# Values of the last two groups of heads by seven half-size products instead of eight

## Chip, core and metric

One core of one Trainium2 chip. The metric is the device time of one execution in microseconds (us), median of the runs shown. Engines: TensorE (PE, with its weight loads as PEld), VectorE (DVE), ScalarE (ACT), GpSimd (POOL), SyncE (SP, which issues most of the DMAs here).

## What is computed

Two layers on a sequence of 512 tokens of width 1024, float32. Layer 0 is a pooling mixer, layer 1 an HGRN2 mixer. Cut to layer 1:

```python
u = h @ w_in                                   # (512, 1024) @ (1024, 8192)
q, fz, i, gate = jnp.split(u, 4, axis=-1)      # each (512, 2048): 16 heads of 128
log_f = jnp.logaddexp(jnp.log(lbf), jnp.log1p(-lbf) + jax.nn.log_sigmoid(fz))
k = (1.0 - lbf) * jax.nn.sigmoid(-fz)
...
o = hgrn2_chunk_scan(qc, kc, vc, bc)           # vc is i, cut into chunks
o = o * lax.rsqrt(jnp.mean(o * o, axis=-1, keepdims=True) + EPS)
...
return (o * jax.nn.silu(gate)) @ w_out
```

`h` is normed before the product; the kernel multiplies by the gain of the norm before it, and by the tokens' factor (`rn`) after it. The values `i` of two groups of heads together are one product of 512 tokens x 1024 inputs by 1024 inputs x 1024 columns.

## The kernel before

Every large product has float32 operands that are split into a high and a low part (`split`, L95 to L97: ACT casts the high part, DVE subtracts it for the low one). Each product of a 128x128 stationary tile and a 128x512 moving tile is then three matmuls (`mm3`, L127 to L130). Weights come in pieces of 512 KB (`piece`, L99 to L107): one DMA on SP's queue into a raw tile `wraw` (three of them, `RAW = 3`), then ACT's cast into `whi` and DVE's subtraction into `wlo` (six pairs, `WB = 6`). A piece holds two of the eight slices of 128 inputs, for 512 columns. These three instructions stand in `tc.high_priority`, so that they are placed some 300 instructions early. The program is a plain list of instructions; a planner orders them for each engine when the program is built, by priority and by its own estimate of when operands and tiles are free, and each engine then runs its list in that order. Tiles with one `tag` share that tag's buffers, and a tile waits until an earlier one with its buffer has had its last reader.

Layer 1 (`hgrn`, L349) works on four groups of four heads (`NG = 4`, `GC = 512` columns a group). For each group:
- `prepare(g)` (L548): `forget` (96 matmuls, with sigmoids and scans of products on DVE) and `queries` (96 matmuls). For each head it ends in a reciprocal on DVE (L572), two products for k on POOL (L574, L575) and two for q on DVE (L576, L577). It runs after the first two heads of the group before have been gated (`gated`, L461), and ahead of the other two.
- `inputs(g)` (L422): the values, in four blocks of 128 tokens, 24 matmuls each (eight slices x three), 96 in all. ACT scales each block by `rn` out of PSUM (L430) into `v` (tag `vn`, one buffer).
- `within` (L580) for each head: four matmuls k by q, a masked copy into `Ads` on DVE (L590, L591), three transposes of k. `state` (L599): three matmuls by `v` and updates on DVE.
- for groups 1 and 2, `add_out` (L381): the output product of the group before, eight halves of 12 matmuls, each added to `ht` on DVE (L379); then `attend` for four heads (L618) and `gates1` (96 matmuls). Group 0 has `turn` (L365, transposes h into `ht`) and the gates around the attention; group 3 has the gates around the attention, and `add_out` of group 2 at its end. `finish` (L503) does the last output product, the norm and the stores.

PSUM has four buffers for the large products (tag `mm`) and four for the small ones (tag `a`). Two groups of small SBUF tiles matter below: `hg` and `sq`, with two buffers each, which sigmoids, gates and norms share; and `f` (two buffers, 2 x 512 elements), which `prepare` holds until its last reciprocal has been used.

```python
def group(g, prepare, heads, zs):
    first, last = g == 0, g == NG - 1
    attend = heads(g, inputs(g))
    ...
    now = [gated(g, n, ons[n], gts[n], last) for n in range(2)]
    if not last:
        prepare(g + 1)
    now += [gated(g, n, ons[n], gts[n], last) for n in range(2, GT)]
    if last:
        add_out(load_out(w1_out, g - 1), zs)
    return now
```

## Time and profile before

| | |
|---|---|
| median of 3 runs | 828.1 us (828.09 to 828.32) |
| profiled execution, device time | 828.94 us |
| its span, first to last instruction | 827.1 us |
| mean granted TensorE clock | 0.997 |
| busy: PE, PEld, DVE, ACT, POOL | 816.1, 685.8, 546.2, 278.7, 150.3 us |
| DMA | 81.14 MB, mean 98 GB/s |

Times of rows are us from the start of the span unless they say ns. A matmul is shown from its start to a modelled end, and the next one begins before that: a run of 128x512 matmuls is to be timed by the distance of the starts. The same holds for DVE and ACT, whose instructions overlap by some 0.1 us.

### The profile page before, as it was taken

To read this page: it belongs to the slowest core of one execution; us is meant where nothing else is said; L and a number is where in the kernel's file an instruction comes from. 1 tells how busy PE (TensorE), PEld (TensorE's weight loads), DVE (VectorE), ACT (ScalarE), POOL (GpSimd) and SP (SyncE) were. 2 spreads that over 40 slices of the span, in tenths; PEclk is the share of its full clock that TensorE was granted. 3 is DMA by queue.
4 is the path that set the end of the run, shared out by engine and by line. 5 is a ranking of instruction groups with operands and counts; after the bars stand their busy time and mean duration, and the time that the engine had idled before them with its cause. 6 is when DMAs were issued, how large, how long until landed. Compare 5 with 4: busy or idle time off the path is not lost.

```text
span 827.1 us, 10198 instructions
## 1 busy us (share of the span) xinstructions
PE 816.1 (99%) x3902; PEld 685.8 (83%) x3902; DVE 546.2 (66%) x837; ACT 278.7 (34%) x476; POOL 150.3 (18%) x197
## 2 busy tenths in 40 slices
PE   9999999999999999999999999999999999999995
PEld 8888888888888888888888888888888888888884
DVE  5687537854785465798169973359973459973744
ACT  7442134223234244325342241343240333242311
POOL 0030010002011032260313400313300313302100
PEclk9999999999999999999999999999999999999998
DMA  9531324223232155133033240333240333240302
GB/s 342 198 103 52 101 102 153 78 71 116 94 101 103 55 178 178 52 102 102 1 102 102 77 128 1 103 102 102 77 128 1 103 101 102 77 126 3 102 14 92
DMA packets 37769, 81.14 MB, mean 98 GB/s; under 512 B 2896, under 2 KB 3152, under 8 KB 37712
## 3 DMA queue, kind: packets, MB, share of 16 engines
q1 hardware_dynamic: 35264, 76.56, 28.3%
q10 hardware_dynamic: 2448, 3.86, 1.3%
q8 instruction: 32, 0.52, 0.3%
q14 instruction: 25, 0.20, 0.1%
HBM read 76.21 MB, written 4.19 MB: 97 GB/s over the span
## 4 chain that ended last, share of the span: by engine, by line
PE 95%; DVE 3%; issue 1%; DMA 0%; ACT 0%; POOLq 0%; POOL 0%; DVEq 0%; ACTq 0%
PE mm L128 29%; PE mm L129 28%; PE mm L130 28%; PE a L625 2%; PE a L627 1%; PE a L588 1%; PE a L605 1%; DVE r L572 1%; PE a L466 1%; DVE wlo L97 1%; PE a L83 1%; PE a L594 0%; DMA wraw<-in_w1i 0%; PE a L128 0%; PE a L130 0%
## 5 line engine op out<-in xcount | busy, mean ns | idle before, releaser
L128 PE MATMUL mm<-xh,whi 128*128 128x512 f32 x624 | 244.7, 392 | 0.0
L129 PE MATMUL mm<-xl,whi 128*128 128x512 f32 x624 | 243.2, 390 | 0.0
L130 PE MATMUL mm<-xh,wlo 128*128 128x512 f32 x624 | 243.0, 390 | 0.0
L96 ACT CAST whi<-wraw 128x1024 fp32r<-128x1024 f32 (+1 forms) x140 | 141.8, 1026 | 237.3 <-PE mm L129 108.6
L97 DVE TENSOR_TENSOR wlo<-wraw,whi 128x1024 fp32r<-128x1024 f32 (+1 forms) x140 | 172.0, 1253 | 56.6 <-ACT whi L96 54.5
L130 PEld LDWEIGHTS mm<-xh,wlo 128*128 128x128 f32 x624 | 117.3, 188 | 24.6
L128 PEld LDWEIGHTS mm<-xh,whi 128*128 128x128 f32 x624 | 117.4, 188 | 24.1 <-DVE h L222 0.3
L129 PEld LDWEIGHTS mm<-xl,whi 128*128 128x128 f32 x624 | 117.3, 188 | 24.2
L572 DVE RECIPROCAL r<-r 128x512 f32<-128x512 f32 x16 | 53.4, 3338 | 0.0
L128 PE MATMUL mm<-whi,xh 128*128 128x512 f32 x128 | 50.1, 391 | 0.0
L129 PE MATMUL mm<-wlo,xh 128*128 128x512 f32 x128 | 50.0, 391 | 0.0
L130 PE MATMUL mm<-whi,xl 128*128 128x512 f32 x128 | 49.9, 390 | 0.0
L129 PE MATMUL mm<-zl,whi 128*128 128x512 f32 x128 | 49.8, 389 | 0.0
L128 PE MATMUL mm<-zh,whi 128*128 128x512 f32 x128 | 49.8, 389 | 0.0
L130 PE MATMUL mm<-zh,wlo 128*128 128x512 f32 x128 | 49.8, 389 | 0.0
L379 DVE TENSOR_TENSOR ht<-mm,ht 128x512 f32<-128x512 f32 x32 | 22.0, 688 | 35.1 <-PE mm L130 35.1
L222 DVE TENSOR_TENSOR h<-mm,h 128x512 f32<-128x512 f32 x32 | 21.9, 688 | 28.4 <-PE mm L130 28.1
L442 POOL TENSOR_TENSOR gs<-fz,s 128x512 f32<-128x512 f32 x16 | 21.5, 1342 | 98.7 <-ACT s L440 98.7
L299 POOL TENSOR_TENSOR gs<-gt,sg 128x512 f32<-128x512 f32 x16 | 21.9, 1372 | 87.8 <-ACT sg L297 87.8
L128 PE MATMUL mm<-whi,z1h 128*128 128x512 f32 x96 | 37.6, 392 | 0.0
L130 PE MATMUL mm<-whi,z1l 128*128 128x512 f32 x96 | 37.4, 390 | 0.0
L129 PE MATMUL mm<-wlo,z1h 128*128 128x512 f32 x96 | 37.4, 389 | 0.0
(151 smaller groups left out, 1156.0 us busy)
## 6 DMA issues: line engine op xcount, KB each, us to landing
wraw<-in_w1i SPq DMA_DIRECT2D x64, 512.0 KB, 3.9
wraw<-in_w0i SPq DMA_DIRECT2D x28, 512.0 KB, 4.3
wraw<-in_w0o SPq DMA_DIRECT2D x16, 512.0 KB, 3.7
wraw<-in_w1o SPq DMA_DIRECT2D x16, 512.0 KB, 4.3
wraw<-in_w0g SPq DMA_DIRECT2D x8, 512.0 KB, 3.9
h<-in_xT SPq DMA_DIRECT2D x8, 256.0 KB, 5.1
wraw<-in_w0i SPq DMA_DIRECT2D x8, 256.0 KB, 5.3
xt<-in_x SPq DMA_DIRECT2D x4, 512.0 KB, 6.7
```

The source lines that it names most:

```text
L83: nc.tensor.matmul(warm[:, :P], ones, ones, start=True, stop=True)
L96: nc.scalar.copy(out=hi, in_=src)
L97: nc.vector.tensor_tensor(out=lo, in0=src, in1=hi, op=ALU.subtract)
L128: nc.tensor.matmul(out, lh, rh, start=start, stop=False)
L129: nc.tensor.matmul(out, lh, rl, start=False, stop=False)
L130: nc.tensor.matmul(out, ll, rh, start=False, stop=stop)
L222: nc.vector.tensor_tensor(out=h[n], in0=acc, in1=h[n], op=ALU.add)
L299: nc.gpsimd.tensor_tensor(out=gs, in0=gt, in1=sg, op=ALU.mult)
L379: nc.vector.tensor_tensor(out=ht[b][:, c], in0=acc, in1=ht[b][:, c], op=ALU.add)
L442: nc.gpsimd.tensor_tensor(out=gs, in0=gt, in1=sg, op=ALU.mult)
L572: nc.vector.reciprocal(out=r, in_=r)
L625: nc.tensor.matmul(o[:, b], Ads[pr][:, j, t], v[:, b, n * P:(n + 1) * P], start=True, stop=b == 0)
```

## The change

For the values of groups 2 and 3 the product X (tokens x inputs) by W (inputs x columns) is cut into 2 x 2 blocks: X into two halves of 256 tokens and two of 512 inputs, W into two halves of inputs and the 512 columns of either group. Seven products of sums of blocks (each two blocks of 128 tokens, four slices of inputs: 24 matmuls) take the place of eight. All seven run in group 2, in `inputs2`; sums of X are made in group 0 (`differences`), written to DRAM, and read back (`again`) into the buffers of `h`; sums of W are made on DVE from raw pieces. The values of group 3 go to DRAM (`v_d`) and `inputs(3)` only reads them. In the last group the output product of group 2 is cut into blocks that stand between the other parts, and half of the gates stand between `within` and `state`. The diff, cut to its core:

```diff
+    h = [const.tile([P, T], F32, name=f"h{k}", tag=f"h{k}", bufs=1) for k in range(KD)]
...
+        own = [[(hi[:, t:t + 256], lo[:, t:t + 256]) for hi, lo in xs[k:k + 4]] for t in (0, 256) for k in (0, 4)]
+        sums_d = dram.tile([2, 4, P, 2, T], F32, name=f"sums_{name}")
+        v_d = dram.tile([TB, P, GC], F32, name=f"v_{name}")
...
+        def differences():
+            for j in range(4):
+                t0, t4 = (small.tile([P, T], F32, name="t", tag="hg", bufs=2) for _ in range(2))
+                for t, k in ((t0, j), (t4, 4 + j)):
+                    nc.scalar.activation(out=t, in_=h[k], func=AF.Copy, scale=pp[:, C_NG1 + k:C_NG1 + k + 1])
+                d, e = (small.tile([P, T], F32, name="d", tag="sq", bufs=2) for _ in range(2))
...
+                first = halves(d, "z1", 4, l1)
+                second = [const.tile([P, T], F32R, name="s", tag=f"h{k}", bufs=1) for k in (j, 4 + j)]
+                split(e, *second)
+                for i, pair in enumerate((first, second)):
+                    for c, x in enumerate(pair):
+                        nc.scalar.dma_start(out=sums_d[i, j, :, c], in_=x.bitcast(F32))
+
+        def again(i):
+            out = []
+            for j in range(4):
+                x = const.tile([P, 2, 256], F32R, name="s", tag=f"h{4 * (i % 2) + j}", bufs=1)
+                nc.sync.dma_start(out=x.bitcast(F32), in_=sums_d[i // 2, j, :, :, (i % 2) * 256:(i % 2) * 256 + 256])
...
+        def inputs2(g):
...
+            def load(*a):
+                raw = wpool.tile([P, 2, GC], F32, name="wraw", tag="wraw", bufs=RAW)
+                with tc.high_priority(AHEAD):
+                    nc.sync.dma_start(out=raw, in_=block(*a))
+                return raw
+            def add(out, x, y):
+                with tc.high_priority(AHEAD):
+                    nc.vector.tensor_tensor(out=out, in0=x, in1=y, op=ALU.add)
+                return out
...
+            def product(accs, x, pieces):
+                for b, acc in enumerate(accs):
+                    t = slice(b * P, (b + 1) * P)
+                    for k, ((xh, xl), (wh, wl)) in enumerate(zip(x, pieces)):
+                        mm3(acc, xh[:, t], xl[:, t], wh, wl, k == 0, k == 3)
+            two = lambda: [ps.tile([P, T], F32, name="mm", tag="mm", bufs=4) for _ in range(2)]
...
+            a = two()
+            product(a, own[0], cut(load(0, 0, 0)) + cut(load(0, 0, 1)))
+            for b in range(2):
+                nc.scalar.copy(out=v[:, 2 + b], in_=a[b])
+            a = two()
+            product(a, own[1], cut(load(1, 0, 0)) + cut(load(1, 0, 1)))
+            for b in range(2):
+                plus(v[:, b], a[b], v[:, 2 + b])
+                times(v[:, b], rn, b)
+            pieces = []
+            for i in range(2):
+                x, y = load(0, 0, i), load(0, 1, i)
+                chain.append(l1.tile([P, 2, GC], F32, name="chain", tag="f", bufs=2))
+                pieces += cut(add(chain[i], x, y))
+            c = two()
+            product(c, s(0), pieces)
+            s2 = s(1)
+            pieces = [x for i in range(2) for x in cut(add(chain[i], chain[i], load(1, 1, i)))]
+            a = two()
+            product(a, s2, pieces)
+            s3 = s(2)
+            for b in range(2):
+                plus(v1[b], a[b], v[:, 2 + b])
+            pieces = []
+            for i in range(2):
+                x, y = load(0, 1, i), load(1, 1, i)
+                pieces += cut(add(x, x, y))
+            a = two()
+            product(a, s3, pieces)
+            s4 = s(3)
+            for b in range(2):
+                plus(v[:, 2 + b], a[b], v1[b])
+                plus(v1[2 + b], c[b], v[:, 2 + b])
+                plus(v1[b], c[b], v1[b])
+                times(v1[2 + b], nrn, 2 + b)
+                nc.scalar.dma_start(out=v_d[2 + b], in_=v1[2 + b])
+            pieces = [x for i in range(2) for x in cut(add(chain[i], chain[i], load(1, 0, i)))]
+            a = two()
+            product(a, own[3], pieces)
+            for b in range(2):
+                plus(v[:, 2 + b], a[b], v[:, 2 + b])
+                times(v[:, 2 + b], rn, 2 + b)
+            a = two()
+            product(a, s4, cut(load(1, 1, 0)) + cut(load(1, 1, 1)))
+            for b in range(2):
+                plus(v1[b], a[b], v1[b])
+                times(v1[b], nrn, b)
+                nc.scalar.dma_start(out=v_d[b], in_=v1[b])
+            return v
...
-            attend = heads(g, inputs(g))
-            if first:
+            v = inputs(g)
+            if last:
+                wg = load_in(w1_in, 3 * DI + g * GC)
+                gts = gates1(wg, (0, 1))
+                attend = heads(g, v, lambda: gts.extend(gates1(wg, (2, 3))))
+                wo = load_out(w1_out, g - 1)
+                add_out(wo, zs, (0,))
+                ons = [attend(n) for n in range(GT)]
+                add_out(wo, zs, (1,))
+            elif first:
+                attend = heads(g, v)
                 turn()
-            if first or last:
+                differences()
...
             if last:
-                add_out(load_out(w1_out, g - 1), zs)
+                add_out(wo, zs, (2, 3))
             return now
...
                 kts = [within(n) for n in range(GT)]
+                if mid:
+                    mid()
                 sts = [state(g, n, kts[n], v) for n in range(GT)]
```

`plus` is a DVE addition of a PSUM tile and an SBUF tile, `times` an ACT scaling in place, `cut` the split of a tile into a `whi` and a `wlo`. In each `j` of `differences` the part left out is four DVE operations on 256 columns.

## Rows read from the trace of the kernel before

**Rows 1.** The page, its busy line and the granted clock in 40 slices.
```profile
PE 816.1 (99%) x3902; PEld 685.8 (83%) x3902; DVE 546.2 (66%) x837; ACT 278.7 (34%) x476; POOL 150.3 (18%) x197
...
PEclk9999999999999999999999999999999999999998
```
**Rows 2.** Waits of PE, 310 to 828 us: total us, times, longest.
```profile
PE a L594 <- ACT kt L596: 0.3, 1, 0.3
PE a L605 <- DVE Ad L591: 0.2, 1, 0.2
```
**Rows 3.** PE in order of time: first and last matmul of group 2's values, 96 in all.
```profile
589.45 0.47 PE L128 MATMUL mm<-whi,xh 128*128 128x512 f32 x1
...
611.33 0.39 PE L130 MATMUL mm<-whi,xl 128*128 128x512 f32 x1
```
**Rows 4.** Stretches: length, busy PE, PEld, DVE, ACT, POOL, clock, DMA share, GB/s.
```profile
567.00:590.00 23.00, 23.00 (x107) 19.12 (x106) 23.00 (x31) 5.27 (x6) 10.88 (x13) 1.00 0.30 92
590.00:612.00 22.00, 22.00 (x100) 18.01 (x99) 17.45 (x18) 7.57 (x10) 3.18 (x2) 1.00 0.33 103
612.00:619.50 7.50, 7.50 (x68) 7.46 (x67) 6.85 (x18) 3.30 (x6) 0.00 (x0) 1.00 0.79 261
619.50:641.00 21.50, 21.50 (x97) 17.75 (x96) 8.83 (x22) 1.87 (x2) 0.00 (x0) 1.00 0.00 1
...
715.00:736.30 21.30, 21.30 (x96) 17.59 (x95) 16.64 (x18) 7.32 (x9) 3.17 (x2) 1.00 0.34 105
```
**Rows 5.** DVE in order of time, 587 to 613 us: start, us, line, operation.
```profile
587.80 3.34 DVE L572 RECIPROCAL r<-r 128x512 f32<-128x512 f32 x1
591.07 3.96 DVE L97 TENSOR_TENSOR wlo<-wraw,whi 128x1024 fp32r<-128x1024 f32 x3
594.95 0.68 DVE L418 TENSOR_TENSOR q<-mm,rb 128x512 f32<-128x512 f32 x1
595.55 0.41 DVE L576 TENSOR_TENSOR q<-q,r 128x256 f32<-128x256 f32 x1
595.88 0.41 DVE L577 TENSOR_TENSOR q<-q,f 128x256 f32<-128x256 f32 x1
596.22 3.34 DVE L572 RECIPROCAL r<-r 128x512 f32<-128x512 f32 x1
599.49 1.15 DVE L97 TENSOR_TENSOR wlo<-wraw,whi 128x1024 fp32r<-128x1024 f32 x1
600.56 0.95 DVE L576 TENSOR_TENSOR q<-q,r 128x256 f32<-128x256 f32 x1
601.44 0.41 DVE L577 TENSOR_TENSOR q<-q,f 128x256 f32<-128x256 f32 x1
601.77 1.40 DVE L468 SCALAR_TENSOR_TENSOR z<-a,pp,gs 128x512 f32<-128x512 f32 x2
603.20 1.35 DVE L97 TENSOR_TENSOR z1l<-z,z1h 128x512 fp32r<-128x512 f32 x2
608.80 3.95 DVE L97 TENSOR_TENSOR wlo<-wraw,whi 128x1024 fp32r<-128x1024 f32 x3 [4.25 <-ACT whi L96]
```
**Rows 6.** The tile `wraw`, 560 to 660 us: from a DMA's issue to its landing.
```profile
DMA to landing us min/median/max: 3.5/3.8/4.7
```
**Rows 7.** ACT in order of time, 595 to 604 us; in brackets the idle time before.
```profile
595.81 1.05 ACT L96 CAST whi<-wraw 128x1024 fp32r<-128x1024 f32 x1 [7.49 <-DMA wraw<-in_w1o]
...
602.55 1.28 ACT L96 CAST z1h<-z 128x512 fp32r<-128x512 f32 x2 [5.10 <-DVE z L468]
603.73 0.69 ACT L430 ACTIVATE vn<-mm,rn_l1fac 128x512 f32<-128x512 f32 x1
```
**Rows 8.** The stretch of group 0's gates and attention (columns as in Rows 4).
```profile
394.00:420.00 26.00, 26.00 (x146) 22.54 (x146) 8.44 (x14) 9.52 (x38) 7.97 (x7) 1.00 0.02 4
```
**Rows 9.** PE in order of time: the transposes after group 0's attention.
```profile
419.64 1.04 PE L466 MATMUL a<-ident,on 128*128 128x128 f32 x8
```
**Rows 10.** The stretch at the end of the span (columns as in Rows 4).
```profile
824.00:827.00 3.00, 0.00 (x0) 0.00 (x0) 0.00 (x0) 0.00 (x0) 0.00 (x0) 0.50 0.03 8
```

More of the change, by code (lines that the diff above doesn't have):

```diff
@@ L91, in trunk @@
     nc.gpsimd.memset(mhalf, -0.5)
-    h = [const.tile([P, T], F32, name=f"h{k}") for k in range(KD)]
     def split(src, hi, lo):
@@ L203, in spread_sbuf, with scaled_halves @@
         return rb
-    def scaled_halves(k, col):
+    def scaled_halves(h, k, col):
         g = pp[:, col + k:col + k + 1]
@@ L347, in trunk, with hgrn @@
     nc.vector.tensor_scalar(out=lb[:, 1], in0=lb[:, 0], scalar1=-1.0, scalar2=1.0, op0=ALU.mult, op1=ALU.add)
-    def hgrn(ctx, general):
+    def hgrn(ctx, general, h):
         name = "gen" if general else "fac"
@@ L357, in hgrn @@
             nc.gpsimd.memset(a, 0.0)
-        xs = [scaled_halves(k, C_NG1) for k in range(KD)]
+        xs = [scaled_halves(h, k, C_NG1) for k in range(KD)]
         accs, rn, rb = project4(load_in(w1_in, DI), xs, lambda: rms(f"l1{name}", h))
@@ L379, in out_half, with add_out @@
             nc.vector.tensor_tensor(out=ht[b][:, c], in0=acc, in1=ht[b][:, c], op=ALU.add)
-        def add_out(pieces, zs):
-            for b in range(TB):
+        def add_out(pieces, zs, blocks=range(TB)):
+            for b in blocks:
                 for half in range(2):
@@ new lines, in again, with block, cut, plus @@
+        def again(i):
[3 more added lines that the diff above has]
+                nc.sync.dma_start(out=x.bitcast(F32), in_=sums_d[i // 2, j, :, :, (i % 2) * 256:(i % 2) * 256 + 256])
+                out.append((x[:, 0], x[:, 1]))
+            return out
+        def inputs2(g):
+            w = w1_in.rearrange("(k p) n -> p k n", p=P)
+            def block(row, col, i):
+                c = 2 * DI + (g + col) * GC
+                return w[:, 4 * row + 2 * i:4 * row + 2 * i + 2, c:c + GC]
+            def load(*a):
[6 more added lines that the diff above has]
+                    nc.vector.tensor_tensor(out=out, in0=x, in1=y, op=ALU.add)
+                return out
+            def cut(x):
+                hi = wpool.tile([P, 2, GC], F32R, name="whi", tag="whi", bufs=WB)
+                lo = wpool.tile([P, 2, GC], F32R, name="wlo", tag="wlo", bufs=WB)
+                with tc.high_priority(AHEAD):
+                    split(x, hi, lo)
+                return [(hi[:, 0], lo[:, 0]), (hi[:, 1], lo[:, 1])]
+            def product(accs, x, pieces):
[4 more added lines that the diff above has]
+            two = lambda: [ps.tile([P, T], F32, name="mm", tag="mm", bufs=4) for _ in range(2)]
+            v = l1.tile([P, TB, GC], F32, name="vn", tag="vn", bufs=1)
+            v1 = [l1.tile([P, GC], F32, name="v1", tag="gs", bufs=4) for _ in range(TB)]
+            chain = []
+            s = again
+            def plus(out, acc, x):
+                nc.vector.tensor_tensor(out=out, in0=acc, in1=x, op=ALU.add)
+            def times(x, by, t):
+                nc.scalar.activation(out=x, in_=x, func=AF.Copy, scale=by[:, t:t + 1])
+            a = two()
[47 more added lines that the diff above has]
+            return v
@@ L422, in inputs @@
         def inputs(g):
-            wi = load_in(w1_in, 2 * DI + g * GC)
+            if g == NG - 2:
+                return inputs2(g)
             v = l1.tile([P, TB, GC], F32, name="vn", tag="vn", bufs=1)
+            wi = load_in(w1_in, 2 * DI + g * GC) if g < NG - 2 else None
             for b in range(TB):
+                if g == NG - 1:
+                    nc.scalar.dma_start(out=v[:, b], in_=v_d[b])
+                    continue
                 acc = ps.tile([P, T], F32, name="mm", tag="mm", bufs=4)
@@ L489, in group @@
             else:
+                attend = heads(g, v)
                 add_out(load_out(w1_out, g - 1), zs)
@@ L492, in group @@
                 gts = gates1(load_in(w1_in, 3 * DI + g * GC), range(GT))
-            if first:
-                l1.tile([P, 32], F32, name="pad2")
             now = [gated(g, n, ons[n], gts[n], last) for n in range(2)]
@@ L730, in weights, with heads @@
                 cur["off"] = offs
-            def heads(g, v):
+            def heads(g, v, mid=None):
+                if mid:
+                    mid()
                 def attend(n):
@@ L759, in trunk @@
     with ExitStack() as c1:
-        marks = hgrn(c1, False)
+        marks = hgrn(c1, False, h)
     in_range = nc.values_load(marks[0:1, 0:1], min_val=0, max_val=P * KI * TB * 3)
     with tc.If(in_range < P * KI * TB * 3), ExitStack() as c1:
+        h = [const.tile([P, T], F32, name=f"h{k}", tag=f"h{k}", bufs=1) for k in range(KD)]
         for k in range(KD):
             nc.sync.dma_start(out=h[k], in_=hmid[k])
-        hgrn(c1, True)
+        hgrn(c1, True, h)
 def _masks():
```

13 lines of the change are left out of this document (10 added, 3 removed).

## The prediction

> **What bounds the kernel now.** I read the page's busy line first: PE is busy for 816 of 827 us, at full clock in every slice but the last [rows 1]. Busy time of a pipelined engine proves little, so the waits of PE come next: in the whole of layer 1 it waited 0.5 us for other engines [rows 2]. So whatever takes a matmul away shortens the kernel, as long as the other engines keep up; and any delay that they add is paid in full. The third view is the stretches, by stage, and there the reader is to see where keeping up is in doubt: in `queries` of group 2 (567 to 590 us) DVE is busy for 23.00 of 23.00 us, and in the values after it for 17.45 of 22.00 [rows 4]. The fourth view is DVE in order of time. PE begins the values at 589.45 [rows 3], but at 591.07 DVE has just ended a reciprocal of `queries` and has another head's to do. The work of `prepare` leaves it only at about 604.5 [rows 5]. In the kernel before this lateness is hidden, because the values need just two more pieces and no vector work of their own. The change puts its vector work exactly there.
>
> **What is removed.** 96 + 96 matmuls become 168, all in group 2. The starts in a steady run stand 0.2267 us apart: the 96 values of group 2 go from 589.45 to 611.55, one step behind the last start [rows 3], 22.1 us with a slow start, 96 x 0.2267 = 21.8 without. 24 fewer are **5.44 us**. Undisturbed, the seven products would end at 611.55 + 72 x 0.2267 = 627.9, the seventh would begin at 622.4, and would want its second piece (third slice of inputs) six matmuls later, at **623.8**.
>
> **What the weights cost DVE.** Price of one 128x1024 subtraction, start to start: three take 3.88 us from 591.07 to 594.95, 1.29 each, with POOL working beside them; the single one at 599.49 takes 1.07 [rows 5]. I take 1.2 and keep 1.07 and 1.29 as ends. The sum of two raw pieces is not in the trace; it has the same shape, two inputs in SBUF and one output, so it gets the same price and ends. The first product's two pieces are cut before, as now. Then come twelve cuts (two for each of products 2 to 7) and eight sums (products 3 to 6): 20 x 1.2 = 24.0 us (21.4 to 25.8).
>
> **What the results cost DVE.** The values leave PSUM on ACT now; in the change there are 14 additions on DVE, 128x512 out of PSUM. Nearest row: q at 594.95, from PSUM and of that size, 0.60 to the next start [rows 5]. Ten of them (two after product 2, two after 4, six after 5) stand before the last cut: 6.0 us.
>
> **What is already there.** Between 591.07 and 604.5, without the four cuts, DVE has 4.5 us (594.95 to 599.49) and 3.9 us (600.56 to about 604.5) to do: 8.5 us [rows 5]. It can't be put off: `chain` takes the buffers of `f`, and the second of these is free only after the last q (601.8), so product 3 waits for the end of `prepare`.
>
> **The sum for DVE.** 8.5 + 24.0 + 6.0 = 38.5 us from 591.07: 629.6. It is wanted at 623.8, so DVE is **5.8 us late** if it never waits (3.2 to 7.6 with the ends above).
>
> **Waits within that.** There are three raw tiles, a load takes 3.8 us (3.5 to 4.7) [rows 6], and a sum of two raw pieces holds two of them. So the second pair's second load of products 3 and 5 is issued only after the first pair's sum, and lands some 4 us later. Going through the slots by hand: y of the second pair of product 3 is issued at about 600.4 and lands at 604.2; DVE has gates' results and additions to fill that. Product 3 gets its second cut at about 607.8 instead of 602. Later DVE stands idle 0.3 to 0.7 us at a time, for a load or for ACT's cast (1.05 us, [rows 7]) between a sum and its cut. I take 1.8 us in all, bounds 0 and 3.
>
> The products would so end 5.8 + 1.8 = 7.6 us late, against 5.44 saved: **+2.2 us**. Against the profiled execution (828.94) that is 831.1, against the median of the runs, 0.84 below it, **830.3**.
>
> **The other parts, mostly at nothing.**
> - SP's queue gets ten more weight loads and 16 reads of sums (256 KB each). Products 2 to 7 want 16 x 0.52 MB in some 40 us, and half of the reads, 2.1 MB, fall there too: with the writes of `v_d` about 290 GB/s. The stretch at 612 shows 261 GB/s at a share of 0.79 [rows 4], so it fits with little room; what it costs is in the 3 us above. The reads for product 5 can be issued only when product 3 has let its sums go, 5.4 us ahead: four transfers on top of 3.8 us, about in time.
> - `differences`: for each j ACT has two scalings and two casts of 512 columns (about 0.6 each, half of the cast in rows 7 and some overhead), DVE 4 x 0.34 (L577, [rows 5]) and two subtractions of 0.6: some 10 us for either engine. It falls in the stretch of 26 us in which they are busy for 8.4 and 9.5 [rows 8]. It holds both buffers of `hg` and `sq`, so gates and norms queue behind it; as one chain it is some 4.3 us for each j, 17 us, to about 411. The norms are due when PE transposes at 419.64 [rows 9]. Cost 0, cover about 3 us; if all of ACT's own 9.5 us stood behind it, 411 + 9.5 is 1 us late.
> - Last group: without values there, PE would reach `within` 21.8 us sooner, but half of the gates (48 matmuls, 10.9 us) stand in front of it, and DVE's tail of `prepare`, some 12 us after `queries` as in group 2, is about covered: the fourth head's matmuls come 3.7 us after the first's. The other half covers the masked copies. The removed four cuts relieve DVE, which is busy 16.64 of 21.3 there [rows 4]. Output product and norms overlap as before. I put it at 0, with 0 to +1.
> - After the seventh product `within` and `state` (7.5 us, DVE 6.85) and the output product (8.83 of 21.5) leave DVE time to catch up [rows 4].
> - ACT's queue: nothing is taken out of order in the row of z1h, which held ACT for 5.10 us while a result of PE waited [rows 7]. If such casts are put ahead of a cast of weights, product 3 is 1 to 3 us later. Not in the sum, in the range.
>
> **Rivals.**
> 1. **DVE keeps pace** (not slower). The place is products 3 to 7. For it: a single cut costs 1.07, and the gates' results z and z1l (2.7 us) aren't wanted before the output product and might be placed after the cuts. Then 35.9 - 2.7 = 33.2 us of work stand against 32.7 to be had, 0.5 us late without waits: 828.1 - 5.4 + 0.5 = **823.2**. It decides from 36.4 us of work and waits down, which is 0.2% faster. Against it: the three in a row at 1.29 from 591.07, three more at the same pace from 608.80 [rows 5], and that z stands ahead of later cuts now.
> 2. **The clock falls.** By the sum, PE stands still for about 4 us in product 3. The granted clock is 1.00 in every stretch with work and 0.50, the lower level of 1.2 GHz, in the last 3 us, after PE had been without work for some 6 us [rows 10]. A product at that clock takes 5.4 us longer, but DVE would catch up by as much as it is late: between 0 and 5.4, up to **835.7**. The Trainium skill (TensorE: Matmul & The Clock Gate, section "Why this matters for your kernels") says that gaps of PE in the middle of a kernel, between bursts of matmuls, bring the half clock back; by it the upper value would hold. No stretch of this trace has such a gap between matmuls.
> 3. **Order in the queues.** ACT's list or group 0's chain in the wrong order: +2 to +3 more, about **833**.
> 4. **It does not take hold**: matmuls saved, but PE waits elsewhere for exactly as much, or the count stays. The diff leaves no way for 192; so only a balance, **828.1**.
>
> **How the numbers follow.** 0.2%, 1.7 us, is about what a measurement of this kernel can tell. The forecast case (DVE late by 5.0 to 10.6 us, 827.7 to 833.3) has 0.50: 0.36 of it slower, 0.14 within. Rival 1, with all of its way up to the forecast (823 to 827.7), 0.30: 0.25 faster, 0.05 within. Rival 2: 0.08, slower. Rival 3: 0.08, of it 0.06 slower and 0.02 within. Rival 4: 0.04, within. That makes faster 0.25, same 0.25, slower 0.50. Both signs hold much; the likeliest case's own range is 827.7 to 833.3. For 8 in 10 I take 824.0 to 835.0.
>
> **What would show it.** In the changed kernel: 24 fewer 128x512 matmuls; DVE busy for over 95% of about 590 to 631; PE waits on `whi` and `wlo`, first and longest in product 3 (some 4 us), then shorter ones up to product 7; the seventh product's end at 634 to 637; the granted clock at 1.00 throughout; the stretch from there to the end 21 to 22 us shorter than before. Wrong would be: DVE with idle time during products 3 to 7 while PE does not wait (rival 1), a clock under 1.00 there (rival 2), waits of the transposes near 420 or in the last group (rival 3).

## The result, and the profile after

The changed kernel takes **840.5 us** (median of four runs, 839.47 to 841.36) against 828.1 before: ratio 1.0149, 95% interval 1.0132 to 1.0167. It is slower by 12.4 us, where 2.2 were forecast and 835 was the end of the range. The profiled execution took 840.38 us, its span 838.6, 11.5 more than before.

The page of the changed kernel, its busy line, the DVE and the clock rows in 40 slices, and the DMA line:
```profile
PE 816.0 (97%) x3878; PEld 682.0 (81%) x3878; DVE 582.5 (69%) x889; ACT 295.1 (35%) x500; POOL 151.4 (18%) x198
...
DVE  5787546844777463997489973279988545995764
...
PEclk9999999999999999999999999999999999999999
...
DMA packets 48299, 96.89 MB, mean 116 GB/s; under 512 B 3696, under 2 KB 8048, under 8 KB 48240
```
PE has 24 instructions fewer than in [rows 1] and is as long busy: a matmul that starts after a wait or at a lower clock is busy for longer (0.50 and 0.77 us against 0.39 in the rows below), so this line doesn't show the loss. The waits of PE in layer 1 (310 to 838 us) show it:
```profile
PE mm L129 <- ACT whi L97: 2.8, 2, 1.6
PE mm L130 <- DVE wlo L98: 2.6, 3, 1.4
PE a L736 <- ACT kt L744: 2.2, 2, 1.8
PE a L753 <- ACT kt L744: 1.0, 2, 0.6
PE a L753 <- DVE Ad L739: 1.0, 1, 1.0
PE mm L129 <- DVE v L502: 0.7, 1, 0.7
PE a L742 <- ACT kt L744: 0.6, 1, 0.6
PE a L736 <- issue: 0.6, 1, 0.6
PE a L736 <- DVE z L608: 0.5, 1, 0.5
```
In [rows 2] the same view had 0.5 us. Here are some 13 with three smaller lines, and the first matmuls after a wait start slowly on top. Where they lie is read from landmarks in PE's list. "Would be" is the distance between two landmarks in the kernel before, plus or minus 0.2267 us for each matmul that was moved or went; "is" is the distance in the changed kernel:

| stretch | would be | is | lost |
|---|---|---|---|
| start of group 0's values to group 2's values (before 357.43 to 589.45, after 356.73 to 593.26) | 232.0 | 236.5 | 4.5 |
| values to the first gated transposes of group 2 (79.55 + 72 matmuls; 593.26 to 698.89) | 95.9 | 105.6 | 9.8 |
| second gated transposes of group 2 to the end of the last group (81.96 - 96 matmuls; 743.35 to 807.76) | 60.2 | 64.4 | 4.2 |

The parts ahead of the first landmark and behind the last each gave back under 1 us. 4.5 + 9.8 + 4.2 less 5.4 saved, less 1.6 at the ends is the 11.5 us of span.

**The products.** PE in order of time, at four of its longest waits:
```profile
604.27 0.42 PE L129 MATMUL mm<-whi,s 128*128 128x512 f32 x1
606.12 0.50 PE L130 MATMUL mm<-wlo,s 128*128 128x512 f32 x1 [1.43 <-DVE wlo L98]
...
607.61 0.40 PE L130 MATMUL mm<-wlo,s 128*128 128x512 f32 x1
609.64 0.50 PE L129 MATMUL mm<-whi,s 128*128 128x512 f32 x1 [1.64 <-ACT whi L97]
...
624.94 0.73 PE L129 MATMUL mm<-whi,s 128*128 128x512 f32 x2 [1.15 <-ACT whi L97]
...
636.84 0.50 PE L129 MATMUL mm<-whi,xh 128*128 128x512 f32 x1 [0.72 <-DVE v L502]
```
The starts stand 1.85 and 2.03 us apart instead of 0.23. The first two are in product 3, as forecast, and then the waits become shorter; the last is not for weights: the second half of product 6 has no PSUM until DVE has added a result (`v`). DVE in order of time:
```profile
598.63 3.34 DVE L720 RECIPROCAL r<-r 128x512 f32<-128x512 f32 x1
601.90 1.15 DVE L479 TENSOR_TENSOR chain<-wraw 128x1024 f32<-128x1024 f32 x1
...
604.20 0.73 DVE L608 SCALAR_TENSOR_TENSOR z<-a,pp,gs 128x512 f32<-128x512 f32 x1
604.86 1.21 DVE L98 TENSOR_TENSOR wlo<-chain,whi 128x1024 fp32r<-128x1024 f32 x1
605.99 0.68 DVE L98 TENSOR_TENSOR z1l<-z,z1h 128x512 fp32r<-128x512 f32 x1
606.59 0.73 DVE L608 SCALAR_TENSOR_TENSOR z<-a,pp,gs 128x512 f32<-128x512 f32 x1
607.25 1.20 DVE L479 TENSOR_TENSOR chain<-wraw 128x1024 f32<-128x1024 f32 x1
...
631.90 2.55 DVE L98 TENSOR_TENSOR wlo<-wraw,whi 128x1024 fp32r<-128x1024 f32 x2
634.37 0.68 DVE L502 TENSOR_TENSOR v<-mm,vn 128x512 f32<-128x512 f32 x1
```
The last reciprocal of `prepare` ends at 601.9 and only then can `chain` take its buffer, as worked out; a cut takes 1.13 from start to start (604.86 to 605.99), a sum 1.08 to 1.15. The last cuts of product 7 end at 634.4. Forecast: 629.6 + 1.8, and 3.8 for the later start, 635.2. But a result of product 5 that PE waits for is added only after them (`v`, 634.37).

The stretches (columns as in [rows 4]):
```profile
593.20:612.00 18.80, 15.74 (x71) 12.45 (x70) 18.73 (x19) 5.60 (x8) 3.18 (x2) 1.00 0.48 149
612.00:636.00 24.00, 21.68 (x113) 17.68 (x112) 20.46 (x22) 11.94 (x15) 0.14 (x2) 1.00 0.91 299
...
755.00:760.00 5.00, 2.99 (x24) 2.50 (x22) 4.77 (x9) 2.04 (x4) 0.75 (x2) 0.99 0.36 105
760.00:765.00 5.00, 4.66 (x26) 4.56 (x27) 3.37 (x9) 2.15 (x5) 2.51 (x2) 0.67 0.01 3
```
DVE is busy 18.73 of 18.80 us up to 612. Behind that the DMAs are busy for 0.91 at 299 GB/s, and DVE stands idle for loads (0.58 and 1.31 us) and for a cast of ACT (1.19) in place of catching up: from 594.6 to 634.4 it is idle for 3.5 us. The clock stays at full speed in the products, but not in the last group.

**Group 0 and the last group.** ACT in order of time, at 378 to 386 and at 757 to 760 us:
```profile
378.08 0.62 ACT L97 CAST z1h<-d 128x512 fp32r<-128x512 f32 x1 [2.41 <-DVE d L439]
...
381.08 0.47 ACT L744 COPY kt<-a 128x384 f32<-128x384 f32 x1
384.18 1.04 ACT L97 CAST whi<-wraw 128x1024 fp32r<-128x1024 f32 x1 [2.63 <-DMA wraw<-in_w1i]
385.13 0.47 ACT L744 COPY kt<-a 128x384 f32<-128x384 f32 x1
385.50 0.72 ACT L435 ACTIVATE t<-h,pp 128x512 f32<-128x512 f32 x1
...
756.97 1.28 ACT L97 CAST z1h<-z 128x512 fp32r<-128x512 f32 x2 [5.64 <-DVE z L608]
759.19 0.63 ACT L580 ACTIVATE s<-fz 128x512 f32<-128x512 f32 x1 [0.95 <-DVE fz L578]
759.73 0.46 ACT L744 COPY kt<-a 128x384 f32<-128x384 f32 x1
```
DVE in order of time, at the same two places:
```profile
376.96 0.41 DVE L438 TENSOR_TENSOR d<-t 128x256 f32<-128x256 f32 x1
...
382.31 0.42 DVE L738 COPY_PREDICATED Ad<-causal,a 64x256 f32<-64x256 uint8 x1
...
755.86 0.41 DVE L725 TENSOR_TENSOR q<-q,f 128x256 f32<-128x256 f32 x1
756.19 1.40 DVE L608 SCALAR_TENSOR_TENSOR z<-a,pp,gs 128x512 f32<-128x512 f32 x2
```
ACT runs its list in order. In group 0 the copies of the transposed k (`kt`) stand behind a cast of the new sums of X that waits 2.41 us for DVE, behind a cast of weights that waits 2.63 us for its load, and behind scalings of the sums; the masked copies (`Ad`) stand behind the first sums in DVE's list. The wait for the load alone is not new. In the kernel before, ACT in order of time:
```profile
382.76 1.04 ACT L96 CAST whi<-wraw 128x1024 fp32r<-128x1024 f32 x1 [1.68 <-DMA wraw<-in_w1i]
```
In the last group the copy of `kt` stands behind casts of `z` that wait 5.64 us for DVE, and DVE reaches `z` only at 756.19, behind the last product for q of `prepare`. PE pays at 381 to 387 and at 760.34 (starts 2.3 us apart, where transposes of a head take 0.3).

Of the 4.5 us of groups 0 and 1, 2.2 are lost by the end of group 0's scores and 0.7 at the transposes of 421 to 425. The other 1.6 come in group 1, most of it at one place: DVE comes to the tail of group 1's `prepare` 3.9 us later than before (a reciprocal at 462.15 against 458.25), and PE waits for a cut of weights. PE in order of time:
```profile
471.32 0.50 PE L130 MATMUL mm<-wlo,xh 128*128 128x512 f32 x1 [0.96 <-DVE wlo L98]
```

### The profile page after: what moved, and what is told of

Read it like the earlier page. It is cut to its first block, busy times and chain, and to the rows that moved or that the text cites. A ratio compares the mean times of both kernels' runs of the same rounds, so it can differ in the third digit from the quotient of the medians.

```text
span 838.6 us, 10334 instructions
## 1 busy us (share of the span) xinstructions
PE 816.0 (97%) x3878; PEld 682.0 (81%) x3878; DVE 582.5 (69%) x889; ACT 295.1 (35%) x500; POOL 151.4 (18%) x198
## 4 chain that ended last, share of the span: by engine, by line
PE 76%; DVE 16%; DMA 3%; issue 2%; ACT 2%; POOL 0%; POOLq 0%; DVEq 0%; ACTq 0%
PE mm L130 23%; PE mm L129 23%; PE mm L131 22%; DVE r L720 4%; DVE wlo L98 4%; DMA wraw<-in_w1i 3%; PE a L775 2%; PE a L777 1%; PE a L753 1%; ACT whi L97 1%; DVE f L705 1%; DVE q L724 1%; DVE f L706 1%; PE a L736 1%; DMA wraw<-in_w1o 1%
## 5 line engine op out<-in xcount | busy, mean ns | idle before, releaser
L594 POOL TENSOR_TENSOR ro<-mo,mhalf 128x4 f32<-128x4 f32 x16 | 16.2, 1014 | 113.1 <-DVE mo L592 113.1
L130 PE MATMUL mm<-wlo,xh 128*128 128x512 f32 x88 | 34.6, 393 | 1.0 <-DVE wlo L98 1.0
L129 PE MATMUL mm<-whi,xh 128*128 128x512 f32 x88 | 34.7, 394 | 0.7 <-DVE v L502 0.7
```

Source lines behind the costliest of these rows:

```text
L129: nc.tensor.matmul(out, lh, rh, start=start, stop=False)
L130: nc.tensor.matmul(out, lh, rl, start=False, stop=False)
L594: nc.gpsimd.tensor_tensor(out=ro[:, :, 0], in0=mo, in1=mhalf[:, :TB], op=ALU.pow)
```

## The experiments

All times are medians, each ratio against the kernel before on the same chip. "The change" is the kernel as given. e4, e7, e8, e11 and e12 leave work out, so that the values of the last two groups are other numbers. The loss of a stretch is read as in the table above, from each run's profiled execution.

| run | us | ratio, 95% interval |
|---|---|---|
| e1 sums of X in group 1 | 842.25 | 1.0165 [1.0149, 1.0182] |
| e2 gates first | 837.95 | 1.0121 [1.0104, 1.0138] |
| e3 sums on GpSimd | 845.90 | 1.0209 [1.0192, 1.0226] |
| e4 no sums of weights | 838.38 | 1.0117 [1.0100, 1.0134] |
| e7 fewer loads | 842.30 | 1.0177 [1.0159, 1.0195] |
| e8 no sums of X | 838.51 | 1.0119 [1.0102, 1.0136] |
| e9 products in group 1 | 843.52 | 1.0187 [1.0170, 1.0204] |
| e10 eight products | 832.77 | 1.0058 [1.0041, 1.0075] |
| e11 seven, no sums at all | 832.78 | 1.0060 [1.0043, 1.0077] |
| e12 sums, few loads | 839.57 | 1.0139 [1.0119, 1.0160] |
| e13 results first | 833.80 | 1.0070 [1.0053, 1.0087] |
| e14 products spread | 830.41 | 1.0027 [1.0018, 1.0037] |
| e15 sums of X after norms | 847.91 | 1.0235 [1.0219, 1.0250] |
| e16 spread, results first | 829.84 | 1.0017 [1.0008, 1.0026] |
| e17 e16, sums of X after norms | 840.52 | 1.0148 [1.0135, 1.0162] |
| e18 e17, kt first | 840.85 | 1.0152 [1.0138, 1.0166] |
| e19 e16, sums of X after one gate | 834.40 | 1.0073 [1.0059, 1.0086] |
| e20 e16, own buffers for sums of X | 833.17 | 1.0056 [1.0043, 1.0070] |

### The last group: e2 and e10

**e2**, the gates as in the kernel before, all ahead of the scores:
```diff
-                gts = gates1(wg, (0, 1))
-                attend = heads(g, v, lambda: gts.extend(gates1(wg, (2, 3))))
+                gts = gates1(wg, range(GT))
+                attend = heads(g, v)
```


> Last group: all four gates stand ahead of the scores (within), two of them no longer behind. Theory A: within comes too early there, while ACT's list holds the copies of k behind casts that wait for DVE's tail of prepare; PE's gaps of 4.2 us in 755 to 764 go, as the gates cover 21.8 us: 840.5 - 4.2 = 836.3 us. Theory B: what is late there is DVE's tail itself and the waits move into the gates or behind them: 839 to 841 us.

2.6 us less than the change. The last group's stretch is 60.75 us, 0.55 from what it would be, and PE is busy for 30.00 of 30.00 us from 740 to 770, where the waits for `z` and `kt` stood. The order that was put at "0, with 0 to +1" cost 3.7 of its 4.2 us by where half of the gates stood.

**e10** keeps only the new order of the last group: eight plain products (24 more matmuls) in group 2, group 3's values by way of DRAM, no sums.
```diff
-                differences()
...
+            for c in (g, g + 1):
+                wi = load_in(w1_in, 2 * DI + c * GC)
+                for b in range(TB):
...
+                    y = v[:, b] if c == g else v1[b]
+                    nc.scalar.activation(out=y, in_=acc, func=AF.Copy, scale=rn[:, b:b + 1])
+                    if c > g:
+                        nc.scalar.dma_start(out=v_d[b], in_=y)
```


> Seven products undone: the values of both groups are made in group 2 as eight plain blocks of 24 matmuls (192), those of the last group go through DRAM as in the change, no sums; the order of the last group is the changed one. Theory A, the new order of the last group has its own price of 4.2 us, whatever comes before: 828.1 + 4.2 = 832.3 us (831 to 833). Theory B, it only shows because VectorE is late from the products: 827.5 to 829 us.

4.7 us slower than the kernel before with every matmul still there. The products lose 0.5 us, the last group 3.4, with the same wait on `kt` of 1.8 us. So moving eight products is free and the new order of the last group is not.

### The products: e4, e7, e12, e11, e3, e13

**e4**, no sums of weights, all loads kept:
```diff
-                pieces += cut(add(chain[i], x, y))
+                pieces += cut(x)
...
-            pieces = [x for i in range(2) for x in cut(add(chain[i], chain[i], load(1, 1, i)))]
+            pieces = [x for i in range(2) for x in cut(load(1, 1, i))]
```
(and the same in the two other products with sums.)

> Leaves out the eight sums of weight pieces: each product takes one block of weights as loaded, with all 18 loads kept, so the values of the last two groups are other numbers. Theory A, VectorE's work bounds the products: 9.2 us less of it, and product 3 no longer waits for the buffers of f; the lateness of 9.8 us falls to about 2 (what the scores among the products cost): 832 to 834 us. Theory B, the loads through three raw tiles bound them: 838 to 841 us.

Only 2.1 us less than the change, though eight instructions of 1.13 us left DVE. The products still lose 8.0 us, now some 5 of them at one place. PE in order of time:
```profile
609.34 0.39 PE L131 MATMUL mm<-whi,s 128*128 128x512 f32 x1
613.25 0.77 PE L129 MATMUL mm<-whi,s 128*128 128x512 f32 x1 [3.52 <-DVE vn L502]
613.81 0.63 PE L130 MATMUL mm<-wlo,s 128*128 128x512 f32 x1
614.24 0.63 PE L131 MATMUL mm<-whi,s 128*128 128x512 f32 x1
```
A result of product 2 is added late, product 4 has no PSUM for 3.5 us, and then the starts stand 0.43 us apart: half the clock, for seven matmuls.

**e7** keeps the sums and takes eight of the 18 loads away, so that ten are left (the second operand is a piece that is there):
```diff
-                x, y = load(0, 0, i), load(0, 1, i)
+                x = load(0, 0, i)
...
-                pieces += cut(add(chain[i], x, y))
+                pieces += cut(add(chain[i], x, x))
```


> Leaves out the ten extra weight loads: where a sum takes a second block of weights it takes the tile at hand twice, so the values of the last two groups are other numbers; VectorE's sums, cuts and additions are all kept, 10 loads are left of 20 in that stage. Theory A, VectorE's list alone (its tail of prepare, then 38 us of work) makes the products late: unchanged, 839.5 to 841.5 us. Theory B, the loads do (rows of the changed kernel show DMA shares of 0.85 to 0.96 at about 300 GB/s from 610 to 640 us, and loads of 4.4 us with up to 5.8): the lateness of 9.8 us falls to 4 to 6 us: 834.5 to 837 us. The run without sums, 838.4, speaks for a share of both.

842.3 us: no gain (its four runs lie between 839.67 and 843.78; the profiled one is the shortest), products 9.1 us late. One gap of 3.7 us for a cast, and again half the clock after it. Neither the loads alone nor the sums alone are the cause; with either gone, the next in the lists is late.

**e11 and e12** take the sums of X away too (own blocks are multiplied in their place), so that group 0 is as before. e11 has neither sums of weights nor second loads, e12 has the sums and few loads.
```diff
-            s = again
+            s = lambda i: own[i]
```


> Seven products of plain blocks: leaves out the sums of weights, the extra loads and the sums of X (values of the last two groups are other numbers); keeps the 14 loads, the 14 additions of results, the order of the last group. It differs from the run of eight plain products, 832.8, by 24 matmuls and the additions. Theory A, sums and loads make the products late: 832.8 - 5.4 + 0.5 to 1.5 = 828 to 829 us. Theory B, they are late because product 3 and 4 stand behind VectorE's tail of prepare in its list (results leave PSUM there) and the scores come among them: 831 to 834 us.

> As the run before, but with the eight sums of weights on VectorE (the second operand is the tile at hand, 10 loads in all). Sums of X and the extra loads stay left out. Against the run without sums, theory A, VectorE's 9.2 us of sums make the products later by 4 to 7 us: 833 to 836. Theory B, the waits for VectorE's tail hide most of them: within 2 us of the run before.

e11 loses 3.2 us in the products, where its only two waits are for results (1.3 and 0.6 us), and the last group's 3.4. e12 is 6.8 us longer: that is what the eight sums cost without a load more. They take 8 x 1.13 = 9.0 us of DVE, and with them come one wait of 3.8 us for a cast in product 3 and a clock of 0.73 to 0.93 from 605 to 625; the three are not told apart.

**e3**, the eight sums on GpSimd:
```diff
-                    nc.vector.tensor_tensor(out=out, in0=x, in1=y, op=ALU.add)
+                    nc.gpsimd.tensor_tensor(out=out, in0=x, in1=y, op=ALU.add)
```


> The eight sums of weight pieces run on GpSimd instead of VectorE. Theory A, VectorE's work bounds the seven products: it loses 8 x 1.15 = 9.2 us there. GpSimd's addition of 128x512 takes 1.34 us in this kernel, so 2.7 us for 1024 columns, 21 us of some 45; the products end 3 to 6 us sooner: 834.5 to 837.5 us. Theory B, the chain load, sum, cast, subtraction through three raw tiles bounds them: each sum is 1.5 us longer in that chain and raw tiles are freed later: 841 to 846 us.

5.4 us worse than the change: products 16.9 us late, gaps of 4.05 and 2.5 us in product 3, and the clock at 0.50 from 610 to 615.

**e13**, e2 and the additions of results placed 600 instructions early:
```diff
-                nc.vector.tensor_tensor(out=out, in0=acc, in1=x, op=ALU.add)
+                with tc.high_priority(2 * AHEAD):
+                    nc.vector.tensor_tensor(out=out, in0=acc, in1=x, op=ALU.add)
```


> The additions that take results out of PSUM get a higher priority than the sums of weights, and the gates stand first in the last group (837.95 alone). Theory A, the results lie in VectorE's list behind sums that wait for loads, and PE waits for PSUM or for v: 1 to 3 us off, 835 to 837. Theory B, PE waits for weights, not for PSUM: 837.5 to 838.5, or later, since cuts move back.

4.15 us less than e2, more than expected. The products lose 6.7 us, the clock is 1.00, and the waits for `v` and `vn` are gone; what is left is product 3's two waits (1.4 and 1.6) and short ones for `wlo`. So some 3 of the 9.8 us were results that stood behind cuts in DVE's list.

### Groups 0 and 1: e8, e1, e15

**e8** leaves out the sums of X, their writes and reads.
```diff
-                differences()
...
-            s = again
+            s = lambda i: own[i]
```


> Leaves out the sums of X, their writes and their reads: the four products that would take them take blocks of X itself, so the values of the last two groups are other numbers; all seven products and the sums of weights are kept. Theory A, the sums' work in group 0 costs 3.8 us there (moved to group 1 it cost 5.5 there): the values of group 2 begin at 589.5 us as before, and the time is 840.5 - 3.8 = 836.7 us. Theory B, the reads of the sums, 4 MB among the weight loads, delay the products as well: 834 to 836 us. Theory C, the waits of group 0 and 1 have another cause: 840 us.

Groups 0 and 1 lose 0.5 us instead of 4.5. So the sums of X cost those 4 us. The time fell by 2.0 only, and that of the profiled execution by 0.8: there the products lost 10.3 instead of 9.8, with a clock of 0.50 from 605 to 610, the last group lost 3.4 instead of 4.2, and 3.6 us went at the ends (group 0's values began 0.85 later, and the span ended 11.7 us after the last matmul instead of 8.9). Why the end took longer is open.

**e1** calls the sums in group 1, ahead of its output product (their high and low parts in a pair of buffers of `f`), **e15** after group 0's norms and gates, with e2's gates:
```diff
                 turn()
-                differences()
...
                 gts += gates1(wg, (2, 3))
+                differences()
```


> The sums of X are made in group 1, ahead of its output product, instead of in group 0 among the masked copies and the attention (one pair of their halves takes a buffer of f in place of two of z1). Theory A, group 0 pays for them: in the changed kernel PE stands 3.8 us later against the kernel before when group 2's values begin (593.26 against 589.45), 2.9 us of it from group 0 on and 1.6 in the values of group 1, less a start that was 0.7 earlier. These go: 840.5 - 3.8 = 836.7 us, and the values of group 2 begin at about 589.5. Theory B, any order of the planner with these extra instructions brings such waits: within 1 us of 840.5.

> The whole change, with the last group's four gates together ahead of the scores (as in the run 'gates first', 837.95 us), and with the sums of X called after group 0's attention and gates instead of before them, so that the masked copies and the norms of group 0 stand ahead of them in DVE's list. Theory A, the 4.5 us that group 0 and group 1 lost came from where the sums were put in the lists and not from their work: the sums now fall in the stretch in which DVE and ACT are free, 3.5 to 4 us come back, 834 to 835 us, and the values of group 2 begin at about 590 instead of 593. Theory B, the work itself (some 10 us for DVE and as much for ACT) costs it wherever it stands in group 0: 837 to 839 us, with the gaps moved to group 1's prepare or values.

e1: group 0 is as before, but group 1's scores wait for `kt` behind casts and scalings (starts 2.2, 1.7 and 1.1 us further apart than without a wait); groups 0 and 1 together lose 6.3 us. The wait went with the sums. e15 is worst of all, by one wait of 10.5 us; e17 (the same move in the spread version) shows it best, below.

### Another place for the products: e9, e14, e16

**e9** puts all seven after group 1's attention, in one piece, with e2's gates.
```diff
+                if g == NG - 3:
+                    held.append(inputs2(g + 1))
```


> The seven products run in group 1, after its output product and attention, where VectorE has no tail of prepare to end; their result waits for group 2; gates of the last group stand ahead of the scores as in the earlier run. Theory A, the products are late because VectorE begins them with the tail of prepare: the lateness of 9.8 us falls to 1 to 3, and 2.6 us come from the last group: 829 to 831.5 us. Theory B, the loads bound them wherever they stand: 836 to 838 us.

843.5: about 9 us are lost up to group 2's scores as well (one gap of 3.3 us for a result, and half the clock behind it), and group 2, with its values done, has nothing to stand in front of its scores: 5.4 us for `z`.

**e14** spreads them: six of the seven products are each followed by a block of group 1's output product or by a gate; gates first in groups 2 and 3. It also puts `v1` into buffers of `kk`.
```diff
+                nxt = next(between, None) if b else None
+                if nxt:
+                    nxt()
...
+                    add_out(wo, zs, (0, 1))
+                    ons = [attend(n) for n in range(GT)]
...
+                    held.append(inputs2(g + 1, [lambda: add_out(wo, zs, (2,)), lambda: add_out(wo, zs, (3,)), *[(lambda n=n: gate(n)) for n in range(GT)]]))
```


> The seven products run in group 1 after the attention, each followed by a block of the output product (two) or one gate (four), so that VectorE has 11 us for each; gates ahead of the scores in groups 2 and 3, to cover the tail of prepare. Theory A, the products are late because their VectorE work is crowded into 38 us: lateness 0 to 2 us; 828.1 - 5.4 + 3.8 (group 0 and 1) + 2 x 1.4 (gates first) + 1 = 830.3, 829 to 832 us. Theory B, single waits on loads and lists stay, wherever the products are: 835 us or more.

> The spread version (products after group 1's attention, between blocks of its output product and its gates, 830.41 us) with the additions of results placed 600 instructions early. Theory A, what is left of the products' 2.6 us is waiting for results behind sums: 829.0 to 830.0 us. Theory B, what is left are the weights' own cuts and the gates' results (the one long gap there ended with fz): within 0.4 us of 830.4.

830.41, as expected: 168 matmuls with 144 of other work between them (two blocks of the output product and four gates, 24 each) give DVE the time it lacks, and group 1 with all its products loses 2.6 us, 1.1 of it at the cut of weights at 470 that the changed kernel waits for too. **e16** (e14 with e13's edit) takes 829.84; the 0.6 us between the two are not clear of noise (the intervals overlap), and group 1 loses 2.7. e16 has the shortest median with seven products, and is still 0.17% above the kernel before (0.08 to 0.26%). It loses 2.9 us in group 0, 2.7 in group 1, 2.6 up to group 2's gated heads (1.5 of it in one wait for a norm) and 0.5 in the last group; 2.0 come back on the way and at the ends. That is 6.7 lost against 5.4 saved. Some 4 of the 6.7 lie where the sums of X cost the changed kernel 4; no run has the spread version without them.

### Sums of X in the spread version: e17 to e20

**e17** is e16 with e15's move; **e18** also places the copies of `kt` 600 instructions early.

> The spread version with results first and with the sums of X after group 0's norms. Theory A, the place of the sums costs 2.5 to 3.5 us in group 0: 826.5 to 828.0 us, at or just below the kernel before (828.1). Theory B, the sums cost the same there: 829.5 to 831 us.

> As the run before it in this list, and the copies of transposed k (kt, ACT) placed 600 instructions early, so that casts of weights that wait for loads stand behind them. Theory A, ACT's list is part of what is left: 0.5 to 1.5 us less than that run, 825.5 to 827.3 us, below the kernel before by more than a measurement can tell. Theory B, the masked copies and DVE are what is left there: within 0.4 us of that run.

Both theories fell: 10.7 us worse, e18 no better. Waits of PE in e17, 430 to 460 us:
```profile
PE mm L129 <- DVE fz L389: 9.5, 1, 9.5
```
DVE in order of time, the first and the last of the four sums, and what stands behind them:
```profile
423.79 0.42 DVE L438 TENSOR_TENSOR d<-t 128x256 f32<-128x256 f32 x1
...
443.98 0.43 DVE L438 TENSOR_TENSOR d<-t 128x256 f32<-128x256 f32 x1 [1.77 <-ACT t L435]
...
448.39 0.68 DVE L98 TENSOR_TENSOR s<-d,s 128x512 fp32r<-128x512 f32 x1
...
451.33 1.28 DVE L389 TENSOR_TENSOR fz<-mm,rb 128x512 f32<-128x512 f32 x2
```
`fz` of group 1's `forget` needs a buffer of `hg`. The sums' chain holds both, from 423.8 to 446, and group 0's `z` takes them next. It takes 5.4 to 9.2 us for each of the four: ACT issues the writes and stands 1.1 to 1.8 us at a pair of them, and in the longest it also casts weights in between. Four blocks of PSUM fill, and PE waits for 9.5 us; the granted clock is 0.60 and then 0.50 from 445 to 455.

**e19** calls them after the first gate, **e20** where the change does; both use the norms' four buffers and write from GpSimd.
```diff
-small.tile([P, T], F32, name="d", tag="sq", bufs=2)
+small.tile([P, T], F32, name="d", tag="sqa", bufs=4)
...
-                        nc.scalar.dma_start(out=sums_d[i, j, :, c], in_=x.bitcast(F32))
+                        nc.gpsimd.dma_start(out=sums_d[i, j, :, c], in_=x.bitcast(F32))
```


> The spread version with results first (829.84 us), and the sums of X called after the first gate of group 0 (behind the masked copies, ahead of the norms), their differences in the four buffers of the norms (sqa) instead of the two of sq, and their writes issued by GpSimd instead of ScalarE. In the run before, the chain of sums held the two buffers of hg from 423 to 450 us, some 5.5 us for each of four, of which ScalarE stood 1.3 to 1.8 us at the issue of the writes. Theory A, with the writes off ScalarE's list the chain takes 3.5 to 4 us for each of four and fits between the first gate (396) and the norms: group 0 loses under 1 us instead of 3.2, 826.8 to 828.2 us. Theory B, the chain is still too long, or holds the gates' buffers: the norms come late and the transposes near 419 wait 3 us or more, 831 to 836 us.

> The same without the move: sums of X where the change has them, but in the buffers of sqa and with their writes issued by GpSimd. Theory A, ScalarE's list (scalings and issues ahead of the kt copies) was the larger part of group 0's 3.2 us: 827.8 to 829.0 us. Theory B, DVE's operations ahead of the masked copies were: within 0.5 us of 829.84.

e19: the chain is 3.54 us for each of four (400.36, 403.90, 407.44, 410.98), as theory A had it, and group 0's scores are nearly clean. But GpSimd, in order of time, now holds the norms:
```profile
420.25 0.54 POOL L447 DMA_DIRECT2D sums_fac<-s  x1
420.81 1.28 POOL L588 TENSOR_TENSOR gs<-fz,s 128x512 f32<-128x512 f32 x1
422.03 1.05 POOL L600 TENSOR_TENSOR ro<-mo,mhalf 128x4 f32<-128x4 f32 x1
```
`mo` was there at 415.5; `ro` (L600) and `gs` stand behind the writes, before three of which GpSimd is idle for 1.9 to 2.4 us, and PE waits 4.5 us. The time is theory B's, by another queue than theory B named. e20 is 3.3 us above e16, where 0 or -1 to -2 was expected; its profiled run (831.29, its shortest) shows group 0 losing 3.6 us instead of 2.9, so writes off ScalarE's list, with the other buffers, gain nothing there. Why its other runs are up to 2 us longer is open.

## Why the prediction was wrong

**What held.** PE was the bound and every delay was paid; 24 matmuls went; the largest term, DVE late after `prepare`, is there with its place (first and longest in product 3), its cause (`chain` after the last q of `prepare`) and its prices: 1.08 to 1.15 for a sum against 1.2, and 0.60 for an addition. e12 against e11 shows the sums alone at 6.8 us. That the last cut ended at 634.4, against 635.2 by the sum, is luck in part: ten additions were to stand before it (6.0 us) and 1.8 us of waits; five did (3.0 us), with 3.5 us of idle time and 1.3 us of masked copies. From 594.6 to 634.4 DVE was busy for 91% and not for over 95%. Rival 1 (DVE keeps pace) fell with them, and no version came near its 823.

**The step that failed is "The other parts, mostly at nothing".** It had 0 for `differences`, 0 (to +1) for the last group and ACT's queue only in the range; measured, groups 0 and 1 lose 4.5 us and the last group 4.2. Of the profiled execution 831.1 us were forecast and 840.4 came: these 8.7, 2.2 more in the products, less 1.6 at start and end.
- `differences`: the work fits into the stretch of [rows 8], and I placed it there because its call stands there. But the planner takes what is ready, and h was: the first of the four stands at 377, ahead of the masked copies and `kt` copies of group 0's scores, with a cast that waits for a load in between. The cover was looked for at 411 to 419, and there the estimate was near: the chain ended at 410, and 0.7 us were lost. But 2.2 us are lost at 381 to 387, and 1.6 in group 1 behind them. e8 shows that the sums cause it. e1, e15, e17 and e19 show that the loss moves with their place: each of the four places tried has something behind it that PE soon needs. That the work alone would be free isn't shown, as no place was.
- Last group: "PE would reach `within` 21.8 us sooner" was seen, and half of the gates were taken as cover for DVE's tail. The tail ended at 756.3, and PE could begin the scores at 755.15; the tail's own results were covered. What was left out is what the tail holds up: `z` stands behind it in DVE's list, the casts of `z` behind that in ACT's, and the `kt` copy behind those. It is the row of [rows 7] that I left out of the sum (z1h, 5.10 us; here 5.64). e10 shows that the order of the last group costs this by itself, and e2 that it goes when all gates stand ahead.

**A term too small: waits within the products.** 7.6 us late was forecast, 9.8 came. The 14 additions had their price but not their place: PE needs PSUM back, and the planner put results behind cuts. With results first (e13) the products are 6.7 late.

**Rival 2 (the clock).** In the products it stayed at 1.00, with waits of 1.85 and 2.03 us from start to start. It fell in the last group: 0.67 from 760 to 765, after PE had stood for 2.0 us. In the experiments it fell in the products of e3, e4, e7 and e12 and in group 1 of e17, where PE had stood for 3.5 us and more, and in e8 to 0.50 from 605 to 610, after waits of 1.93 and 1.77 us from start to start. The Trainium skill (TensorE: Matmul & The Clock Gate, "Why this matters for your kernels") has it that gaps between bursts bring the half clock back; the trace agrees for these, while in e10 PE stood 2.0 us at the same place as in the changed kernel and the clock stayed at 1.00 (the last group lost 3.4 us there, against 4.2). The clock is a part of why e4 and e7, which relieve DVE or the DMAs, gave so little: they turned several short waits into one long one, and in e4 the slow matmuls after it cost another 1.4 us.

**Rival 3 (order in the queues)** is what happened, beside the forecast and not in its place, and at some three times its price (8.7 against 2 to 3 us): I let it exclude the main term, and gave it 0.08.

## What to carry over

A change that saves 1% of a fully busy engine has to be checked against every in-order list that it adds to: for each added instruction ask not when its engine has time, but where the planner can put it as soon as its operands are there, and what PE needs that then stands behind it. Terms of that kind in several places add up; they are no alternatives to each other or to the main term. Work that another engine has to keep up with is best spread among work that needs little from it (e14 against e9), and where results crowd, what frees PSUM goes ahead of what feeds the next product (e13; in the spread version, e16, the gain is not clear of noise).

## What was not expected of the hardware

- The same gap gave both clocks: PE stood 2.0 us for `kt` in the last group of the changed kernel, of e4 and of e10; the clock was 0.67, 0.67 (both from 760 to 765) and 1.00 (750 to 760). In product 3, two waits of some 2 us left it at 1.00 in the changed kernel and were followed by 0.50 in e8.
- After a gap of 3.5 us (e4) seven matmuls stood 0.43 us apart before 0.2267 came back, some 1.4 us lost on top of the gap.
- A write issued by GpSimd took 0.54 to 0.78 us of its list in e19; a pair issued by ACT took 1.1 to 1.8 in e17. The Trainium skill (GPSIMD Engine Reference, "When to use GPSIMD") says that GpSimd itself generates the descriptors of such DMAs; the trace agrees in so far as they stand in its list as work.
